# Low halves of the U blocks ahead of the gates: from GpSimd to VectorE

## The chip, the core and the metric

One NeuronCore of a Trainium2 chip runs the whole program. The metric is device time in microseconds (us). The engines are TensorE (PE, with its weight loads shown apart as PEld), VectorE (DVE), ScalarE (ACT), GpSimd (POOL) and SyncE (SP), which issues most of the DMAs. Each engine takes its instructions in the order in which they were placed on it.

## The reference, cut to what matters

One decoder layer over 512 tokens of width 1024: a token mixer (differential attention beside a gated linear recurrence), then PEER, a channel mixer that picks 128 experts per token out of 16384 by product keys. Only the second part matters here:

```python
q = jnp.einsum('nd,dc->nc', xb, w_query).reshape(PEER_BLOCK, PEER_HEADS, 2, PEER_QUERY_DIM // 2)
s = jnp.einsum('nhpc,hpkc->nhpk', q, subkeys).astype(jnp.float32)
sv, si = lax.top_k(s, PEER_TOPK)
...
top_s, pos = lax.top_k(cand_s, PEER_TOPK)
experts = jnp.take_along_axis(cand_i, pos, axis=-1).reshape(PEER_BLOCK, PEER_HEADS * PEER_TOPK)
gates = jax.nn.softmax(top_s, axis=-1).reshape(PEER_BLOCK, PEER_HEADS * PEER_TOPK)
u = u_table[experts]
hid = jax.nn.gelu(jnp.einsum('nkd,nd->nk', u, xb).astype(jnp.float32), approximate=False) * gates
return jnp.einsum('nk,nkd->nd', hid.astype(xb.dtype), v_table[experts])
```

## The kernel before

For the first three blocks of 128 tokens (ND = 3, 384 tokens) PEER is computed densely: all 16384 experts, in 128 blocks of 128 rows of U and V, with a dense matrix of gates that is zero where an expert was not picked. The last block of 128 tokens gathers its experts' rows instead.

fp32 products are made of three matmuls (`mm3`, L110 to L112) over operands that are split into a high and a low half. `split` (L105) lets ACT write the high half (L106) and VectorE or, where an engine is passed, that engine the low half (L107): `lo = src - hi`. `u_piece` loads 128 x 1024 numbers into `ur` (L655, SP's queue) and splits them into `uh` and `ul`; `ur`, `uh` and `ul` have three buffers each.

The part of the program around the change has these stages:

1. **Queries** (`s` from 0 to 15): TensorE multiplies a 128-column piece of the query weights (`ps_q`; these pieces are split with GpSimd), then scores (`pss`); VectorE picks the 16 largest of each list (`top16`, L736 to L740); GpSimd adds pairs of lists (`cand`, L763).
2. **Run-ahead and gates**: hidden values of the first 40 U blocks (RING = 40) are computed "ahead", in quarter steps (`run_ahead`, HP = 4), between the pieces of routing (`route`, L790 to L827) and the gate matmuls (`gates4`). A block is 24 matmuls into `ps_h` (two PSUM buffers), then a gelu on ACT into `hr` (L698). `gates4` makes two groups of one-hots on VectorE (`oh`, L837 and L843, three buffers), eight matmuls into `pgt` (L850, L851), and an ACT copy into `stg` (L852); there are 96 calls, 32 for each token block, and four steps of run-ahead go with five calls (RATE = 0.8). `stg` is stored to `g_dram`.
3. **Dense stage**: for each of 128 blocks the gates are read back (`gsl`, L975), a V block is loaded (`vr`, L977) and split, `hr` is multiplied by the gates (L982) and split (`wh`, `wl`), and 18 matmuls add into `y`; the hidden values of block `i + 40` follow. These U blocks are split with VectorE. VectorE also works on the gathered rows here (L912, L928).

A scheduler decides the order of instructions on each engine, from the program's order, the tiles' buffers and its own costs; only VectorE's order in the dense stage is the program's. Below, "gate" means one call of `gates4`, "block" one U block (24 matmuls), and "UL" one low half of a ring block (L107, `ul<-ur,uh`, 128x1024). UL0 is that of block 0.

Of the kernel before, what the change touches and what calls it, by code (L numbers as in the profile page):

```python
# [20 lines left out]
P = 128  # L21
# [16 lines left out]
ND = 3  # L38
# [2 lines left out]
GS = 2.0 ** 14  # L41
GB = 32
GI = 4
# sums of a pair of descending lists that can be among the 16 largest:
# (first row, rows, columns) of the blocks that cover (a + 1) * (b + 1) <= 16
CBLK = [(0, 1, 16), (1, 1, 8), (2, 2, 5), (4, 4, 3), (8, 8, 1)]
NCAND = sum(n * m for _, n, m in CBLK)
RING = 40
HP = 4
# [11 lines left out]
def tile_kernel(  # L61
# [25 lines left out]
    V, S, G, PE = nc.vector, nc.scalar, nc.gpsimd, nc.tensor  # L87
# [10 lines left out]
    V.memset(nhalf, -0.5)  # L98

    def rstd(dst, ssq, n, width):  # L100
        """dst = (ssq / n + eps) ** -0.5 for [P, width] tiles."""
        G.tensor_scalar(dst, ssq, 1.0 / n, EPS, op0=OP.mult, op1=OP.add)
        G.tensor_tensor(dst, dst, nhalf[: dst.shape[0], :width], op=OP.pow)

# [6 lines left out]
        PE.matmul(ps, ah, bl, start=False, stop=False)  # L111
        PE.matmul(ps, al, bh, start=False, stop=last)  # L112

    # ------------------------------------------------------------------ front
    with ExitStack() as fr:
        rstack = fr.enter_context(ExitStack())
        pa = fr.enter_context(tc.tile_pool(name="pa", bufs=8, space=PSUM))
# [4 lines left out]
        ssq = mixp.tile([P, NTB, 8], F32, name="ssq")  # L122
# [3 lines left out]
        with ExitStack() as pr:  # L126
# [35 lines left out]
            first = [pp.tile([P, HALF], F32, name="ps_t", tag="pa") for _ in range(4)]  # L162
# [56 lines left out]
                    f, *a = steps.pop(0)  # L219
                    f(*a)  # L220

            # ---- HGRN2 projections
            Q, QF, KR, FF = [], [], [], []
            w_second = w_piece(1)
            for xr in XR:
# [5 lines left out]
            second = [proj_t(w_second, 0, lo, hi) for lo, hi in halves]  # L231
# [20 lines left out]
            PE.transpose(prm, rv[:NMETA, NTB : NTB + 1].to_broadcast([NMETA, P]), ident[:NMETA, :NMETA])  # L252
            V.tensor_copy(rb[:, :NMETA], prm)

            # gates' lower bound: softmax over the two rows of logits, first row
            lg = fc.tile([P, 2, NH], F32, name="lg")
            nc.sync.dma_start(lg, lbl)
            lmx = fc.tile([P, NH], F32, name="lmx")
# [10 lines left out]
            for pc in range(2):  # L269
                for cb in range(2):  # L270
# [13 lines left out]
                    V.tensor_scalar(k, f, -1.0, 1.0, op0=OP.mult, op1=OP.add)  # L284
                    FF.append(f)
                    KR.append(k)
            # lambda
            lq = fc.tile([P, 4, 64], F32, name="lq")
            nc.sync.dma_start(lq.rearrange("p a b -> p (a b)"), row_bcast(lqk, 256))
            lsum = fc.tile([P, 2], F32, name="lsum")  # L290
# [29 lines left out]
            for pc in range(2):  # L320
                w = w_piece(2 + pc)
                for cb in range(2):
# [8 lines left out]
                    V.tensor_tensor(qf, q, FF[h][:, NMETA:], op=OP.mult)  # L331
                    Q.append(q)
                    QF.append(qf)
            # ---- HGRN2: scores inside the chunks, by a tree of decays
            AT = [hg.tile([P, NTB, P], F32, name=f"at{h}") for h in range(NH)]
            TOT = [(FF[h], NMETA) for h in range(NH)]

# [39 lines left out]
                run_one(vsteps)  # L377
            va, vam, vsteps = natural(12, "va", hp_)

            # ---- HGRN2: states at the chunks' starts and outputs  # L380
            def keys(h):
                k = KR[h]
                pk = pm.tile([P, 4, P], F32, name="pk", tag="pa")
# [47 lines left out]
            hstack.close()  # L431
            aqp = pr.enter_context(tc.tile_pool(name="aqp", bufs=1, reuse_waits="tile"))

            # ---- attention projections
            AQ, AK = [], []
            for which, lst, lo in ((8, AQ, NMETA), (10, AK, 0)):
                for pc in range(2):
                    w = w_piece(which + pc)
                    for cb in range(2):
                        n = T - lo  # L440
                        raw = tp.tile([P, T], F32, name="raw", tag="w2", bufs=W2)
                        segs = [(lo, T)] if n <= 512 else [(0, HALF), (HALF, T)]
                        for a, b in segs:
                            ps = proj_t(w, cb, a, b)
                            S.activation(raw[:, a - lo : b - lo], ps, AF.Copy, scale=0.125 if lo else 1.0)
                        rot = tp.tile([P, T], F32, name="rot", tag="w2", bufs=W2)
                        for g in range(4):
                            src = (g ^ 1) * 32
                            nc.sync.dma_start(rot[g * 32 : g * 32 + 32, :n], raw[src : src + 32, :n])
                        hh = pc * 2 + cb  # L450
                        V.tensor_tensor(rot[:, :n], rot[:, :n], sinr[:, lo:], op=OP.mult)
                        if lo:
                            # one query of the pair per half, zeros in the other
                            r = aqp.tile([P, 2, SEQ], F32, name=f"aq{hh}")
                            G.memset(r[64:, 0], 0.0)
                            G.memset(r[:64, 1], 0.0)
                            V.tensor_tensor(raw[:, :n], raw[:, :n], cosr[:, lo:], op=OP.mult)
                            for p2 in range(2):
                                r0 = slice(p2 * 64, p2 * 64 + 64)
                                V.tensor_tensor(r[r0, p2], raw[r0, :n], rot[r0, :n], op=OP.add)  # L460
                        else:
                            r = hp_.tile([P, T], F32, name=f"ak{hh}", tag=f"f{hh}")
                            V.tensor_tensor(r, raw, cosr, op=OP.mult)
                            V.tensor_tensor(r, r, rot, op=OP.add)
                        lst.append(r)
            # ---- attention core
            def scores(h, tb):
                nk = NMETA + (tb + 1) * P
                segs = [(0, nk)] if nk <= 512 else [(0, HALF), (HALF, T)]
# [57 lines left out]
                junk2 = tp.tile([P, P], F32, name="junk2", tag="junk2")  # L527
                S.activation(junk2, po, AF.Square, accum_out=ssq[:, tb, h : h + 1])

            # gate of the recurrence, times the norm's weight  # L530
            wg = {}

            def rg_step(i, tb):
# [108 lines left out]
            s1(SP)  # L642
            run_one(F)

        # ------------------------------------------------------ output projection
        xbp = ctx.enter_context(tc.tile_pool(name="xbp", bufs=1, reuse_waits="tile"))
        xbn_ = xbp.tile([P, D], F32, name="xbn")
        xbn_box.append(xbn_)
# [24 lines left out]
        s2(SP, 1)  # L673
        s3(2, X.pop(2), pm, "pa")

    # --------------------------------------------------------------- PEER
    ringp = ctx.enter_context(tc.tile_pool(name="ringp", bufs=RING, reuse_waits="tile"))
    ph = ctx.enter_context(tc.tile_pool(name="ph", bufs=2, space=PSUM, reuse_waits="tile"))
    spp = ctx.enter_context(tc.tile_pool(name="spp", bufs=1))
# [5 lines left out]
            pieces[i] = u_piece(uT[i], eng)  # L685

    def h_parts(i, eng=None, n=1):
        """gelu of block i's hidden values, in n steps; the last one appends it to the ring"""
        h_load(i, eng)
        if eng is not None and i + 1 < RING:  # L690
            h_load(i + 1, eng)
        uh, ul = pieces.pop(i)
        ps = ph.tile([P, DTOK], F32, name="ps_h", tag="ph")
        for kc in range(KC):
            mm3(ps, uh[:, kc], ul[:, kc], xbh[:, kc, :DTOK], xbl[:, kc, :DTOK], kc == 0, kc == KC - 1)
            if kc == KC - 1:
                hr = ringp.tile([P, DTOK], F32, name="hr", tag="hr")
                S.activation(hr, ps, AF.Gelu)  # L698
                ring.append(hr)
            if (kc + 1) % (KC // n) == 0:  # L700
                yield
# [3 lines left out]
    ring = []  # L705

    with ExitStack() as rt:
# [12 lines left out]
        starts = rc.tile([P, 16], I16, name="starts")  # L720
# [21 lines left out]
        for s in range(NSET):  # L742
            wh, wl = u_piece(wq[s], G) if s else qw_first
            ps = pq.tile([P, SEQ], F32, name="ps_q", tag="pq")
            parts = [slice(0, 256), slice(256, SEQ)] if s == 0 else [slice(0, SEQ)]
# [12 lines left out]
            if s % 2 == 1:  # L758
# [3 lines left out]
                for a0, na, nb in CBLK:  # L762
# [4 lines left out]
                        op=OP.add,  # L767
# [4 lines left out]

        qs.close()
        rw = rt.enter_context(tc.tile_pool(name="rg", bufs=2, reuse_waits="tile"))
        steps = (None for i in range(RING) for _ in h_parts(i, G, HP))

        def run_ahead(n):
            for _ in range(n):
                next(steps, None)

        def route(tb):
            # experts' two key indices
            idx = []

            def pick(which, sel, op, key, table, dt):
                """idx of the selected key: sum over a of op(sel, key[a]) * table[a]"""
                eq = rw.tile([P, PH * TOPK, TOPK], dt, name="eq", tag="eq", bufs=1)
                full = [P, PH * TOPK, TOPK]
                S.activation(eq, sel.rearrange("p h k -> p (h k)").unsqueeze(2).to_broadcast(full), AF.Copy)
                V.tensor_tensor(eq, eq, key.unsqueeze(1).to_broadcast(full), op=op)  # L790
                eqh = eq.rearrange("p (h k) a -> p h k a", h=PH)
                V.tensor_tensor(eqh, eqh, table.unsqueeze(2).to_broadcast([P, PH, TOPK, TOPK]), op=OP.mult)
                for w in (8, 4, 2):
                    V.tensor_tensor(eq[:, :, :w], eq[:, :, :w], eq[:, :, w : 2 * w], op=OP.add)
                ix = rw.tile([P, PH, TOPK], U32 if dt == I16 else F32, name=f"ix{which}")
                V.tensor_tensor(ix.rearrange("p h k -> p (h k)"), eq[:, :, 0], eq[:, :, 1], op=OP.add)
                return ix

            # first list: rank a is the last one whose candidates start at or before the position;
            # 64 * key + start comes out as a sum of the table's steps  # L800
            comb = rw.tile([P, PH, TOPK], I16, name="comb", bufs=1)
            step = rw.tile([P, PH, TOPK], I16, name="step", bufs=1)
            V.scalar_tensor_tensor(
# [10 lines left out]
            rank = rw.tile([P, PH, TOPK], F16, name="rank", bufs=1)  # L814
# [3 lines left out]
            idx = [ixa, pick(1, rank, OP.is_equal, io16, sif, F16)]  # L818
# [11 lines left out]
            return pmj  # L830

        def gates4(pmj, t0, stg, c0):
            """dense gates of four tokens: one-hots of the first key, of it times the gate's two parts, of the second"""
            oh = rw.tile([P, 4, P, 4], F16, name="oh", bufs=3)
            pgt = pg.tile([P, 4, P], F32, name="pgt", tag="pg")
            tq4 = slice(t0, t0 + 4)
# [4 lines left out]
                op=OP.is_equal,  # L841
# [5 lines left out]
                op=OP.mult,  # L847
# [4 lines left out]
            S.activation(stg[:, :, c0 : c0 + 4].rearrange("p i t -> p t i"), pgt, AF.Copy)  # L852

        run_ahead(16)
        # gates, in two parts of 11 bits for the dense blocks
        fl = "p t h k -> p (t h) k"
        mx = rc.tile([P, NTB * PH], F32, name="mx")
        V.tensor_copy(mx, TSA[:, :, :, 0].rearrange("p t h -> p (t h)"))
# [35 lines left out]
        for i in range(RING, RING + 1):  # L894
            h_load(i, G)

    # dense part for the first ND token blocks, gathered part for the last
    with ExitStack() as dn:
        dp = dn.enter_context(tc.tile_pool(name="dp", bufs=2, reuse_waits="tile"))
        gp = dn.enter_context(tc.tile_pool(name="gp", bufs=4, reuse_waits="tile"))  # L900
# [61 lines left out]
        last = []  # L962
        for i in range(NK):
# [31 lines left out]
            last = []  # L995
# [75 lines left out]
```

## Time and profile before

| what | value |
|---|---|
| three runs | 1656.32, 1657.58 (median), 1660.24 us |
| span of the profiled execution | 1655.8 us (median less span: 1.8 us) |
| busy over the span | PE 1595.0, DVE 1246.4, ACT 672.6, POOL 566.7 us |
| first ring matmul / first gate matmul / first `y` matmul | 441.56 / 517.13 / 751.38 us |

PE's busy time is a union of pipelined matmuls: one ring matmul is shown as about 334 ns long, while the next starts about 0.173 us after it. So PE's load is read from starts, not from busy time. PEclk is the granted clock of TensorE as a share of 2.4 GHz; its other level, 1.2 GHz, is 0.5.

### The profile page before, as it was taken

The page shows a single profiled execution, that of the slowest core. Times are in us where ns is not written, and L with a number is a line of the kernel's source. Part 1 is how long each engine was busy: PE and PEld are TensorE (multiplying, and loading weights), DVE is VectorE, ACT ScalarE, POOL GpSimd, SP SyncE. Part 2 cuts the span into 40 slices and gives each one's busy share as a digit, 9 for nine tenths or more (in the row PEclk, how much of TensorE's full clock was granted, in tenths as well). Part 3 has the DMA queues.
Part 4 walks back from the last instruction along what each step waited for, and adds up shares of the span by engine and source line. Part 5 has one row for each costly group of instructions (what it writes and reads, how often), then busy time and mean ns, then how long its engine had stood idle before and what let it go on. Part 6 is the DMA issues. An engine that isn't in the chain of part 4 may idle for free.

```text
span 1655.8 us, 23775 instructions
## 1 busy us (share of the span) xinstructions
PE 1595.0 (96%) x8859; PEld 1427.1 (86%) x8859; DVE 1246.4 (75%) x2375; ACT 672.6 (41%) x1017; POOL 566.7 (34%) x429
## 2 busy tenths in 40 slices
PE   7999998999978889999999999999999999999997
PEld 7899986888777889898999999999999999988886
DVE  6772568568898897837877778777777777767776
ACT  5123265422245666753433333333333333323333
POOL 2000012334444223254444444444444444433221
PEclk9999999999988999999999999999999999999999
DMA  6211322322222354569999988998898999877884
GB/s 205 77 50 45 118 71 103 115 90 77 73 81 100 143 203 174 207 228 357 337 322 319 324 306 308 318 323 309 311 331 304 318 321 314 311 233 262 282 278 144
DMA packets 145635, 363.93 MB, mean 220 GB/s; under 512 B 11888, under 2 KB 61296, under 8 KB 145392
## 3 DMA queue, kind: packets, MB, share of 16 engines
q1 hardware_dynamic: 107936, 227.10, 39.4%
q0 software_dynamic: 37008, 134.27, 23.4%
q8 instruction: 69, 1.13, 0.3%
q10 hardware_dynamic: 576, 1.05, 0.2%
q14 instruction: 46, 0.38, 0.1%
HBM read 330.92 MB, written 29.36 MB: 218 GB/s over the span
## 4 chain that ended last, share of the span: by engine, by line
PE 80%; DVE 13%; ACT 2%; DMA 1%; issue 1%; POOL 1%; SPq 0%; POOLq 0%; DVEq 0%; ACTq 0%
PE y L112 10%; PE y L111 10%; PE y L110 10%; PE ps_h L112 9%; PE ps_h L110 9%; PE ps_h L111 9%; PE pgt L850 2%; DVE oh L837 2%; PE pgt L851 2%; DVE oh L843 2%; PE ps_t L110 2%; PE ps_l L342 2%; PE ps_t L112 2%; PE ps_t L111 2%; PE ps_n L110 1%; PE ps_n L111 1%
## 5 line engine op out<-in xcount | busy, mean ns | idle before, releaser
L110 PE MATMUL ps_h<-xbh,uh 128*128 128x384 f32 x1024 | 355.1, 347 | 9.1 <-ACT hr L698 9.1
L112 PE MATMUL ps_h<-xbh,ul 128*128 128x384 f32 x1024 | 348.3, 340 | 3.3 <-POOL ul L107 3.3
L111 PE MATMUL ps_h<-xbl,uh 128*128 128x384 f32 x1024 | 347.6, 339 | 0.0
L110 PE MATMUL y<-vh,wh 128*128 128x512 f32 x768 | 299.0, 389 | 3.2 <-ACT wh L106 3.0
L112 PE MATMUL y<-vh,wl 128*128 128x512 f32 x768 | 300.9, 392 | 0.0
L111 PE MATMUL y<-vl,wh 128*128 128x512 f32 x768 | 300.4, 391 | 0.0
L922 POOL DMA_INDIRECT vg<-in_v_dram,exp_idx x128 | 185.3, 1448 | 277.8 <-DVE acc L928 210.6
L908 POOL DMA_INDIRECT ug<-in_u_dram,exp_idx x128 | 177.5, 1387 | 215.7 <-DVE jk L912 151.2
L107 DVE TENSOR_TENSOR vl<-vr,vh 128x1024 fp32r<-128x1024 f32 x128 | 156.8, 1225 | 123.0 <-ACT vh L106 121.1
L106 ACT ACTIVATE vh<-vr 128x1024 fp32r<-128x1024 f32 x128 | 136.0, 1062 | 266.2 <-issue 215.2
L106 ACT ACTIVATE uh<-ur 128x1024 fp32r<-128x1024 f32 x144 | 152.7, 1062 | 158.8 <-issue 69.4
L107 POOL TENSOR_TENSOR ul<-ur,uh 128x1024 fp32r<-128x1024 f32 x57 | 151.2, 2658 | 191.9 <-ACT uh L106 191.9
L110 PEld LDWEIGHTS ps_h<-xbh,uh 128*128 128x128 f32 x1024 | 197.2, 193 | 13.7 <-ACT hr L698 10.1
L111 PEld LDWEIGHTS ps_h<-xbl,uh 128*128 128x128 f32 x1024 | 196.3, 192 | 3.5
L112 PEld LDWEIGHTS ps_h<-xbh,ul 128*128 128x128 f32 x1024 | 195.3, 191 | 3.6 <-POOL ul L107 3.6
L110 PEld LDWEIGHTS y<-vh,wh 128*128 128x128 f32 x768 | 144.2, 188 | 31.9 <-ACT wh L106 4.2
L112 PEld LDWEIGHTS y<-vh,wl 128*128 128x128 f32 x768 | 144.1, 188 | 31.1 <-DVE wl L107 0.9
L111 PEld LDWEIGHTS y<-vl,wh 128*128 128x128 f32 x768 | 144.1, 188 | 28.3
L106 ACT ACTIVATE wh<-hr 128x384 fp32r<-128x384 f32 x128 | 67.2, 525 | 246.4 <-DVE hr L982 241.7
L928 DVE SCALAR_TENSOR_TENSOR acc<-vg,hid,acc 128x1024 f32<-128x1024 f32 x127 | 162.7, 1281 | 3.3 <-DMA vg<-in_v_dram,exp_idx 1.4
L912 DVE SCALAR_TENSOR_TENSOR jk<-ug,xbn 128x1024 f32<-128x1024 f32 x128 | 156.4, 1222 | 8.9 <-DMA ug<-in_u_dram,exp_idx 6.5
L107 DVE TENSOR_TENSOR wl<-hr,wh 128x384 fp32r<-128x384 f32 x128 | 71.5, 559 | 83.7 <-ACT wh L106 83.1
(268 smaller groups left out, 2716.5 us busy)
## 6 DMA issues: line engine op xcount, KB each, us to landing
ur<-in_uT_dram SPq DMA_DIRECT2D x128, 512.0 KB
vr<-in_v_dram SPq DMA_DIRECT2D x128, 512.0 KB
g_dram<-stg SPq DMA_DIRECT2D x48, 512.0 KB
gsl<-g_dram SPq DMA_DIRECT2D x32, 768.0 KB
wr<-in_w_in_dram SPq DMA_DIRECT2D x26, 512.0 KB
ur<-in_wq_dram SPq DMA_DIRECT2D x16, 512.0 KB
wor<-in_w_out_dram SPq DMA_DIRECT2D x8, 512.0 KB
xr<-in_xT_dram SPq DMA_DIRECT2D x8, 264.0 KB
```

The source lines that it names most:

```text
L106: S.activation(hi, src, AF.Copy)
L107: (eng or V).tensor_tensor(lo, src, hi.bitcast(F32), op=OP.subtract)
L110: PE.matmul(ps, ah, bh, start=first, stop=False)
L111: PE.matmul(ps, ah, bl, start=False, stop=False)
L112: PE.matmul(ps, al, bh, start=False, stop=last)
L342: PE.matmul(ps[:, c, :], KR[h][:, cs], rhs[:, c * P : c * P + P], start=True, stop=True)
L837: V.tensor_tensor(oh[:, :2], io128.unsqueeze(1).to_broadcast([P, 2, P, 4]), pmj[:, :2, tq4].unsqueeze(2).to_broadcast([P, 2, P, 4]), op=OP ...
L843: V.tensor_tensor(oh[:, 2:], oh[:, 0:1].to_broadcast([P, 2, P, 4]), pmj[:, 2:, tq4].unsqueeze(2).to_broadcast([P, 2, P, 4]), op=OP.mult,)
L908: G.indirect_dma_start(out=ug, out_offset=None, in_=u, in_offset=bass.IndirectOffsetOnAxis(ap=exp_idx[:, k : k + 1], axis=0))
L912: V.scalar_tensor_tensor(jk, ug, 1.0, xbn_, op0=OP.mult, op1=OP.mult, accum_out=hid[:, k : k + 1])
L922: G.indirect_dma_start(out=vg, out_offset=None, in_=v, in_offset=bass.IndirectOffsetOnAxis(ap=exp_idx[:, k : k + 1], axis=0))
L928: V.scalar_tensor_tensor(acc, vg, hid[:, k : k + 1], acc, op0=OP.mult, op1=OP.add)
```

## The change

`h_parts` no longer takes GpSimd for the 40 blocks that are run ahead, so `split` falls back to VectorE for their low halves. The test that loads and splits block `i + 1` before block `i` is multiplied hung on the engine that was passed; it now hangs on the number of steps (`n > 1`), so that the run-ahead keeps its look-ahead. The query pieces and block 40 stay on GpSimd, and the dense stage is as before. The other differences are removed comments.

```diff
     def h_parts(i, eng=None, n=1):
...
         h_load(i, eng)
-        if eng is not None and i + 1 < RING:
+        if n > 1 and i + 1 < RING:
             h_load(i + 1, eng)
...
-        steps = (None for i in range(RING) for _ in h_parts(i, G, HP))
+        steps = (None for i in range(RING) for _ in h_parts(i, None, HP))
```

Forty instructions leave GpSimd's queue and forty join VectorE's; the scheduler also places other work differently. VectorE's order at the end of the last `top16` and the start of routing (`tsa`: the scores' top 16, later the gates; `comb`, `step`, `eq`: routing's tables) was before:

```order
L858 COPY mx<-tsa 128x32
L739 MAX tsa<-t_4722 128x8
L740 MAX_INDEX ti_3463<-tsa,t_4722 128x8
L860 TENSOR_TENSOR tsa<-tsa,mx 128x512
L803 SCALAR_TENSOR_TENSOR comb<-si_3458,starts 128x128
...
L790 TENSOR_TENSOR eq<-eq,starts 128x2048
L792 TENSOR_TENSOR eq<-eq,step 128x2048
L794 TENSOR_TENSOR eq<-eq 128x128x8
```

and is now, at the same place:

```order
L107 TENSOR_TENSOR ul<-ur,uh 128x1024
L739 MAX tsa<-t_4722 128x8
L858 COPY mx<-tsa 128x32
L740 MAX_INDEX ti_3463<-tsa,t_4722 128x8
L107 TENSOR_TENSOR ul<-ur,uh 128x1024
L860 TENSOR_TENSOR tsa<-tsa,mx 128x512
...
L792 TENSOR_TENSOR eq<-eq,step 128x2048
L107 TENSOR_TENSOR ul<-ur,uh 128x1024
L794 TENSOR_TENSOR eq<-eq 128x128x8
```

These are UL4, UL5 and UL6. UL0 and UL1 stand in the two `top16` groups ahead of the last query pair, UL2 and UL3 at the end of that of `s = 15`, and UL7 to UL13 between the steps of routing; 14 ULs stand ahead of the first gate's one-hots, where there was none.

ACT's order at the same time (`hr` is the gelu that frees a PSUM buffer of TensorE, `eq` a copy that routing on VectorE waits for) was before:

```order
L698 ACTIVATE hr<-ps_h 128x384
L789 ACTIVATE eq<-ti_3463 128x2048
L106 ACTIVATE uh<-ur 128x1024
L698 ACTIVATE hr<-ps_h 128x384
L106 ACTIVATE uh<-ur 128x1024
L698 ACTIVATE hr<-ps_h 128x384
L861 ACT_TABLE_LOAD
```

and is now:

```order
L698 ACTIVATE hr<-ps_h 128x384
L106 ACTIVATE uh<-ur 128x1024
L698 ACTIVATE hr<-ps_h 128x384
L789 ACTIVATE eq<-ti_3463 128x2048
L106 ACTIVATE uh<-ur 128x1024
L698 ACTIVATE hr<-ps_h 128x384
L861 ACT_TABLE_LOAD
```

One high half and one gelu moved ahead of the first `eq`. On PE, 313 ring matmuls (13.04 blocks) now stand ahead of the first gate matmul instead of 264 (11 blocks), and five instead of six blocks follow the last gate.

In the gates, VectorE's order just after the sixteenth one-hot group of the first token block, where routing of the second is made, was before:

```order
L843 TENSOR_TENSOR oh<-oh,pmj 128x1024
L813 CAST ixa<-k_5518 128x128
L815 TENSOR_TENSOR rank<-ti_3461,ix_5516 128x128
L837 TENSOR_TENSOR oh<-io_3432,pmj 128x1024
L806 COPY step<-comb 128x8
L807 TENSOR_TENSOR step<-comb 128x8x15
L843 TENSOR_TENSOR oh<-oh,pmj 128x1024
L837 TENSOR_TENSOR oh<-io_3432,pmj 128x1024 x2
L790 TENSOR_TENSOR eq<-eq,io_3431 128x2048
```

and is now:

```order
L843 TENSOR_TENSOR oh<-oh,pmj 128x1024
L794 TENSOR_TENSOR eq<-eq 128x128x8
L107 TENSOR_TENSOR ul<-ur,uh 128x1024
L794 TENSOR_TENSOR eq<-eq 128x128x4
L107 TENSOR_TENSOR ul<-ur,uh 128x1024
L794 TENSOR_TENSOR eq<-eq 128x128x2
L107 TENSOR_TENSOR ul<-ur,uh 128x1024
L796 TENSOR_TENSOR ix_5516<-eq 128x128
L837 TENSOR_TENSOR oh<-io_3432,pmj 128x1024
L810 TENSOR_SCALAR k_5518<-ix_5516 128x128
L843 TENSOR_TENSOR oh<-oh,pmj 128x1024
```

The first half of this routing now comes behind the sixteenth group, with three ULs in it, and its second half runs between the next five gates instead of ahead of them. Everywhere else in the gates one UL stands between an L837 and its L843, once for about five gates.

## Rows read from the trace of the kernel before

**Rows 1.** Stretches around the ring: us and instructions of PE, PEld, DVE, ACT, POOL; PEclk; DMA

```profile
441.00:517.00 76.00, 57.15 (x280) 55.00 (x278) 66.72 (x240) 29.99 (x32) 33.20 (x22) 0.82 0.23 77
517.00:751.00 234.00, 219.71 (x1474) 203.15 (x1472) 179.15 (x225) 147.62 (x160) 83.58 (x33) 0.99 0.52 190
550.00:570.00 20.00, 15.87 (x90) 14.86 (x90) 15.47 (x18) 9.42 (x10) 7.72 (x3) 0.83 0.51 181
590.00:620.00 30.00, 25.71 (x181) 23.16 (x180) 26.71 (x34) 18.10 (x20) 7.58 (x3) 1.00 0.52 193
751.00:1656.00 905.00, 895.37 (x4416) 800.18 (x4416) 706.37 (x877) 333.20 (x455) 363.81 (x264) 1.00 0.86 301
```

**Rows 2.** Waits of PE, 440 to 750: total us, times, longest

```profile
PE ps_h L110 <- ACT hr L698: 9.1, 3, 5.3
PE pgt L850 <- DVE oh L843: 7.5, 16, 1.6
PE ptp L827 <- DVE ixa L813: 6.5, 1, 6.5
PE ptp L827 <- DVE ix L796: 4.1, 1, 4.1
```

**Rows 3.** The tile ul: ns min/median/max, first and last start

```profile
L107 DVE TENSOR_TENSOR ul<-ur,uh x87: 1210/1218/1221, 758.3 to 1466.0; 128x1024 fp32r<-128x1024 f32 x87
L107 POOL TENSOR_TENSOR ul<-ur,uh x57: 2343/2412/5164, 312.8 to 742.5; 128x1024 fp32r<-128x1024 f32 x57
```

**Rows 4.** Timeline of VectorE, 470 to 515: start, us, what, [idle before <-releaser]

```profile
470.81 3.28 DVE L792 TENSOR_TENSOR eq<-eq,step 128x2048 int16<-128x2048 int16 x1
...
505.99 1.22 DVE L792 TENSOR_TENSOR eq<-eq,sif 128x2048 f16<-128x2048 f16 x1
507.25 0.69 DVE L794 TENSOR_TENSOR eq<-eq 128x1024 f16<-128x1024 f16 x1
...
514.25 3.48 DVE L843 TENSOR_TENSOR oh<-oh,pmj 128x1024 f16<-128x1024 f16 x2
```

**Rows 5.** Timeline of GpSimd, VectorE and ACT, 448 to 476

```profile
448.20 2.34 POOL L107 TENSOR_TENSOR ul<-ur,uh 128x1024 fp32r<-128x1024 f32 x1
450.84 0.34 DVE L736 MAX8 tsa<-cand 128x8 f32<-128x54 f32 x2 [1.93 <-POOL cand L763]
467.61 1.91 ACT L789 ACTIVATE eq<-ti 128x2048 int16<-128x2048 uint32 x1 [9.03 <-DVE ti L740]
470.55 5.77 POOL L107 TENSOR_TENSOR ul<-ur,uh 128x1024 fp32r<-128x1024 f32 x2 [4.23 <-ACT uh L106]
```

**Rows 6.** Timeline of a steady stretch of the gates: GpSimd, VectorE, PE

```profile
666.46 2.89 POOL L107 TENSOR_TENSOR ul<-ur,uh 128x1024 fp32r<-128x1024 f32 x1 [6.46 <-ACT uh L106]
667.35 2.55 DVE L837 TENSOR_TENSOR oh<-io,pmj 128x1024 f16<-128x1024 f16 x1 [0.25 <-PE pgt L851]
668.22 0.29 PE L850 MATMUL pgt<-oh 128*128 128x128 f16 x1
...
670.56 0.28 PE L850 MATMUL pgt<-oh 128*128 128x128 f16 x1 [0.17 <-DVE oh L843]
...
672.56 0.28 PE L850 MATMUL pgt<-oh 128*128 128x128 f16 x1
...
675.77 2.90 POOL L107 TENSOR_TENSOR ul<-ur,uh 128x1024 fp32r<-128x1024 f32 x1 [6.42 <-ACT uh L106]
```

**Rows 7.** Timeline of PE: first of a group of three ring matmuls, and three groups on

```profile
479.89 0.33 PE L110 MATMUL ps_h<-xbh,uh 128*128 128x384 f32 x1
...
481.45 0.33 PE L110 MATMUL ps_h<-xbh,uh 128*128 128x384 f32 x1
```

**Rows 8.** Timeline of the ring's end: VectorE, ACT, PE

```profile
719.81 0.69 DVE L843 TENSOR_TENSOR oh<-oh,pmj 128x1024 f16<-128x1024 f16 x1
...
747.50 1.06 ACT L106 ACTIVATE vh<-vr 128x1024 fp32r<-128x1024 f32 x1 [6.13 <-DMA vr<-in_v_dram]
751.38 0.50 PE L110 MATMUL y<-vh,wh 128*128 128x512 f32 x1 [3.03 <-ACT wh L106]
```

## The prediction

> **What bounds the kernel now.** I read the busy times by stage first. From 751 us to the end TensorE is busy 895.4 of 905 us at full clock [rows 1]: that stage is TensorE's own, the change doesn't touch its code, and a microsecond won before it reaches the end whole. So only the stretch from the first ring matmul (441.6) to the first `y` matmul (751.4, [rows 8]) counts: 309.8 us.
>
> How much of it is work? Three groups of three ring matmuls take 481.45 - 479.89 = 1.56 us [rows 7], so a block (eight groups) is 8 x 0.52 = 4.16 us and 40 blocks are 166.4. In the steady gates one period, from one low half on GpSimd to the next, is 675.77 - 666.46 = 9.31 us [rows 6] and holds five gates and one block: (9.31 - 4.16) / 5 = 1.03 us a gate, 98.9 for 96. That leaves 309.8 - 265.3 = 44.5 us, of which I put some 5 on scores and transposes. About 40 us are lost. The windows say where: TensorE sits idle 76 - 57.2 = 18.8 us before the first gate and 234 - 219.7 = 14.3 behind it, and ahead of the first gate its mean clock is 0.82, so some 0.36 of that time lies at 1.2 GHz [rows 1].
>
> Then I asked who is waited for. TensorE waits 9.1 us for gelu copies on ACT, 6.5 and 4.1 for routing results of VectorE, and 7.5 in 16 pieces for one-hots [rows 2]. The first is VectorE's too: ACT's `eq` copy stood 9.03 us waiting for the top 16 [rows 5], with the gelus behind it in ACT's queue. So before the gates VectorE's chain (top 16, softmax, routing) ends last; in the steady gates TensorE does.
>
> And VectorE's chain is slowed by GpSimd. The multiplication at L792 took 3.28 us beside GpSimd's low halves (470.55, for 5.77 us) and 1.22 at 505.99, the sum at L794 0.69 when nothing ran there [rows 4, 5]. In the gates, L837 took 2.55 us and ended at 669.90, 0.55 behind the low half that had begun at 666.46; the usual one-hot takes 0.69 [rows 6, 8]. A low half on GpSimd costs VectorE nearly 2 us when they meet. The Trainium skill says why (SBUF — State Buffer, Who interferes with whom): a VectorE instruction with two SBUF inputs shares a read port with GpSimd and waits for the whole of an instruction there. The trace agrees.
>
> **The change, part by part.** A low half takes 1.22 us on VectorE and 2.41 (median) on GpSimd [rows 3]. Forty of them add 40 x 1.22 = 48.8 us to VectorE and take 40 x 2.41 = 96 from GpSimd, which is not waited for in the end. What counts is what they displace.
>
> *Ahead of the first gate.* 14 ULs join VectorE's chain: +17.1 us. What goes: seven instructions between 470 and 517 that met GpSimd (first and last: L792 at 470.81, the pair L843 at 514.25 with 3.48 against 2 x 0.69). Their excess is 3.28 - 1.22 = 2.06 for the first and 3.48 - 1.38 = 2.10 for the last [rows 4, 8], so about 7 x 2.1 = 14.7. Also the 1.93 us in which VectorE waited for `cand`, queued behind a low half [rows 5]; GpSimd has only `cand` there now. Balance: 17.1 - 14.7 - 1.9 = +0.5 us. One new wait comes in: UL5 needs `uh5`, which needs block 2 off its buffer, and UL2 and UL3 are made only when the last `top16` is nearly over, so TensorE has nothing between blocks 1 and 2, and `hr2` now stands ahead of the first `eq` on ACT. I put +1.5 us on it: the `eq` can start about when block 2 is evicted. The first gate then comes at about 519 instead of 517.1. But by then 13.04 blocks are multiplied, not 11: 2.04 x 4.16 = 8.5 us of TensorE's work is out of the way. Can they be fed? From the first `eq` (467.6) to the first gate nine ULs are made in about 50 us, one for 5.5 us, slower than the 4.16 that TensorE needs, but with blocks 2 to 4 in hand. Term: -8.5 + 2 = **-6.5 us**. Bounds: the first gate 1.5 us earlier than before (if the ACT wait falls into time in which VectorE waited for ACT anyway), -10; if those long instructions are not shortened at all, 14.7 more: +8.2.
>
> *Routing of the second token block* (550 to 570). Here TensorE lost 20 - 15.9 = 4.1 us, and the clock of 0.83 over 20 us [rows 1] means 0.34 of it, 6.8 us, at the lower level, half of that lost: 3.4. Together 7.5. Now five gates stand between the two halves of this routing. I count VectorE from the sixteenth one-hot to the `ixa` that TensorE waits for: sums 0.69 + 0.45 + 0.42, three ULs 3.66, two results 0.43 + 0.67, one gate 1.38, in all 7.7; TensorE has one gate and 1.12 blocks, 1.03 + 4.66 = 5.7, so it waits 2.0. Term: 7.5 - 2.0 = **-5.5**. Bounds -7.5 and 0.
>
> *Routing of the third* (590 to 620): 30 - 25.7 = 4.3 lost [rows 1]. By the same count, VectorE has 10.3 us to the next `ixa` (two multiplications 2.44, two ULs 2.44, sums 1.56, two gates 2.76, the results 1.1), and TensorE one gate and 1.8 blocks, 8.5: it waits 1.8. Term: **-2.5**, bounds -4.3 and 0.
>
> *Steady gates.* A period with a low half loses a little each time: from 668.22 to 670.56 a gate and a quarter block take 2.34 us, from 670.56 to 672.56 without it 2.00 [rows 6]. 0.34 x 20 periods = 6.8. The UL now delays the same one-hots, by 1.22 where it was 2.55 - 0.69 = 1.86. VectorE then needs 5 x 1.38 + 1.22 = 8.1 us of a period of 9.0, and each UL's high half stands several gates ahead of it on ACT. I take half: **-3**; bounds -6.8 and 0.
>
> *Ring's end.* VectorE ended the last one-hots at 720.5, `y` began at 751.4: 31 us, of which TensorE waited the last 3.03, because `vr` landed only at 747.5 [rows 8]. Five blocks (20.8 us) instead of six follow now. The loads stand behind the same stores, but the `ur` loads ahead of them on SP no longer wait for low halves at GpSimd's pace, since VectorE has nothing else there. I take **0**; bounds -3 (the wait goes) and +4 (one block less to hide the loads, nothing gained).
>
> Sum: -6.5 - 5.5 - 2.5 - 3 + 0 = -17.5 us. The profiled execution has 1655.8 us of span, 1.8 below the median of the runs; 1655.8 - 17.5 + 1.8 = 1640.1. I say **1640**. Behind 751 nothing is to be won: VectorE's and GpSimd's order there is the same.
>
> **Rivals.** *A. VectorE becomes the bound, slower.* It is busy 66.7 of 76 us ahead of the first gate [rows 1], and the new instructions stand in its one queue, where everything behind them waits. If the long instructions are long for another reason than GpSimd, the first gate comes 8.2 + 8.5 = 16.7 us late, and the two blocks won give 8.5 back: 1657.6 + 8.2 = 1666. It decides from the point at which less than about 6 of the 14.7 us of excess go away. Against it: short and long cases of the same instruction stand 35 us apart, and differ in whether GpSimd was at work [rows 4, 5]. The Trainium skill speaks for this rival (Perfetto Trace Analysis, Optimizing Scalar/DVE Operations): a saturated VectorE is to be relieved, even towards GpSimd; the same paragraph warns that the two share a read port. By the first half the change costs, by the second it doesn't; the traces favour the second. 15%.
>
> *B. Given back at the ring's end.* If the loads of the dense stage keep their 31 us from the last one-hots, the blocks won early only make TensorE wait there: five blocks and a gate are 21.8 us, six were 26, so 4.2 go: 1644; and if routing still holds the gates back as before (no -5.5, no -2.5), 1652. For it: `y` already waits 3 us. 15%, around 1650.
>
> *C. Hidden anyway.* GpSimd is not the bound, and the new waits of VectorE for ACT's high halves eat the steady and routing terms, and as much again in the first: 1656 to 1658. For it: ACT holds gelus, `eq` and high halves in one queue, and once waited 9 us there [rows 5]. 10%.
>
> *D. More.* If blocks are fed so well that the lower clock vanishes too, the 0.36 x 76 = 27 us at 1.2 GHz give back another 8 or so beyond the terms: 1631. Against it: UL2 comes late. 10%.
>
> **How the numbers follow.** The forecast, 50%, has its own range of 1633 to 1650. With D's 1631 inside and C's 1658 and about a third of A reached, 8 in 10 lie in 1630 to 1660. 0.2% is 3.3 us, about what a measurement of this kernel can tell from no change. Faster: the forecast, D and B, 75%; same: C, 10%; slower: A, 15%.
>
> **What would show it.** In the changed profile: GpSimd without `ul` between 436 and 742 but for block 40; L792, L794 and L837 without lengths of 2.5 us and more; `ul` on VectorE at about 1.22; the first gate matmul at 517 to 521 with 313 ring matmuls ahead of it; TensorE's busy time around the two routings at 9 of 10 or more; `y` at 730 to 738. I am wrong if VectorE stands waiting for ACT's `uh` ahead of its ULs, if TensorE's clock ahead of the gates falls well below 0.82, or if `y` waits for `vr` by much more than 3 us.

## The result, and the profile after

The changed kernel takes 1633.99 us (median; 1632.69 to 1634.34), the kernel before 1656.95 on the same chip (1655.16 to 1660.24): 0.986 of it, 95% interval 0.9847 to 0.9873. The span is 1632.6 us after 1655.8, and nearly all of the gain lies ahead of the first `y` matmul: it starts at 729.99 instead of 751.38 us, 21.4 earlier. The last 1.8 us come behind it.

The busy times by stage, of the changed kernel (columns as in [rows 1]: window, its length, busy us of PE, PEld, DVE, ACT, POOL, granted clock, DMA share, GB/s):

```profile
441.00:515.00 74.00, 60.21 (x331) 58.45 (x330) 66.18 (x252) 33.80 (x37) 3.28 (x10) 0.93 0.29 100
512.00:706.00 194.00, 189.36 (x1310) 175.53 (x1309) 160.28 (x250) 137.61 (x146) 0.00 (x0) 0.98 0.48 177
520.00:550.00 30.00, 27.70 (x181) 25.59 (x180) 25.29 (x42) 19.00 (x21) 0.00 (x0) 0.89 0.39 151
550.00:570.00 20.00, 20.00 (x140) 18.54 (x140) 16.90 (x27) 16.84 (x19) 0.00 (x0) 1.00 0.44 158
590.00:620.00 30.00, 29.37 (x204) 27.69 (x202) 27.00 (x44) 19.94 (x21) 0.00 (x0) 1.00 0.54 200
...
525.00:530.00 5.00, 3.70 (x29) 3.23 (x27) 4.46 (x7) 3.07 (x5) 0.00 (x0) 0.76 0.33 129
530.00:535.00 5.00, 5.00 (x26) 4.53 (x24) 2.96 (x5) 2.69 (x3) 0.00 (x0) 0.56 0.98 358
```

TensorE idles 13.8 us ahead of the first gate, where it was 18.8, at a clock of 0.93 for 0.82; the two holes of the routings (15.87 of 20 and 25.71 of 30 in [rows 1]) are closed. VectorE is busy for 66.2 us ahead of the first gate, as before (66.7), though it makes 14 low halves more. A new hole stands at 520 to 550, at a clock of 0.89, most of which belongs to the ten microseconds of the last two lines. The second line, from the first to the last one-hot, is read further below.

The tiles `oh` and `ul` of the changed kernel (ns min/median/max, first and last start):

```profile
L850 PE MATMUL pgt<-oh x384: 274/297/330, 514.5 to 708.9; 128*128 128x128 f16 x192
L837 DVE TENSOR_TENSOR oh<-io,pmj x96: 669/685/705, 512.5 to 703.3; 128x1024 f16<-128x1024 f16 x96
L843 DVE TENSOR_TENSOR oh<-oh,pmj x96: 672/684/706, 513.7 to 705.0; 128x1024 f16<-128x1024 f16 x96
...
L107 DVE TENSOR_TENSOR ul<-ur,uh x127: 1201/1218/1228, 442.7 to 1443.2; 128x1024 fp32r<-128x1024 f32 x127
L107 POOL TENSOR_TENSOR ul<-ur,uh x17: 2371/2392/2420, 312.2 to 722.2; 128x1024 fp32r<-128x1024 f32 x17
```

None of 192 one-hots is long any more. The same lines of the kernel before say what they were, and how long the gates took:

```profile
L850 PE MATMUL pgt<-oh x384: 275/297/302, 517.1 to 722.9; 128*128 128x128 f16 x192
...
L837 DVE TENSOR_TENSOR oh<-io,pmj x96: 673/686/2823, 513.0 to 719.1; 128x1024 f16<-128x1024 f16 x96
L843 DVE TENSOR_TENSOR oh<-oh,pmj x96: 667/684/2884, 514.2 to 719.8; 128x1024 f16<-128x1024 f16 x96
```

So the first gate is 2.6 us earlier, the stretch from the first to the last gate 194.4 us instead of 205.8 (-11.4), and from the last gate to `y` it is 21.1 instead of 28.5 (-7.4): together the 21.4.

TensorE's waits from 440 to 740 (total us, times, longest), to be read against [rows 2]; the waits for one-hots are gone, and a new one leads:

```profile
PE ps_h L112 <- DVE ul L107: 12.4, 3, 9.4
PE ps_h L110 <- ACT hr L698: 5.3, 7, 1.3
PE ptp L827 <- DVE ixa L813: 1.1, 1, 1.1
PE ptp L827 <- DVE ix L796: 0.3, 1, 0.3
```

The timeline of the changed kernel has the place of the 9.4 us: UL2, the low half of the third block, is made only at 462.41, behind a `top16`, and that block's first matmul that needs it (L112) waits until then. The first `eq`, which the prediction saw coming when block 2 is evicted, starts at 471.66.

```profile
462.41 1.21 DVE L107 TENSOR_TENSOR ul<-ur,uh 128x1024 fp32r<-128x1024 f32 x1
463.68 0.69 PE L112 MATMUL ps_h<-xbh,ul 128*128 128x384 f32 x1 [9.41 <-DVE ul L107]
...
470.32 1.06 ACT L106 ACTIVATE uh<-ur 128x1024 fp32r<-128x1024 f32 x1 [14.38 <-PE ps_h L111]
471.42 1.22 DVE L107 TENSOR_TENSOR ul<-ur,uh 128x1024 fp32r<-128x1024 f32 x1 [1.72 <-ACT uh L106]
471.66 1.90 ACT L789 ACTIVATE eq<-ti 128x2048 int16<-128x2048 uint32 x1
```

### The profile page after: what moved, and what is told of

Same layout as the page of the kernel before. It is cut to its first block, busy times and chain, and to the rows that moved or that the text cites. A ratio compares the mean times of both kernels' runs of the same rounds, so it can differ in the third digit from the quotient of the medians.

```text
span 1632.6 us, 23785 instructions
## 1 busy us (share of the span) xinstructions
PE 1586.8 (97%) x8859; PEld 1422.3 (87%) x8859; DVE 1230.8 (75%) x2415; ACT 673.7 (41%) x1017; POOL 457.6 (28%) x389
## 4 chain that ended last, share of the span: by engine, by line
PE 87%; DVE 7%; ACT 3%; POOL 1%; issue 1%; DMA 1%; SPq 0%; POOLq 0%; DVEq 0%; ACTq 0%
PE ps_h L110 11%; PE y L111 11%; PE y L112 11%; PE ps_h L112 11%; PE y L110 11%; PE ps_h L111 10%; PE pgt L850 3%; PE pgt L851 3%; PE ps_t L110 2%; PE ps_l L342 2%; PE ps_t L112 2%; PE ps_t L111 2%; PE ps_n L110 2%; PE ps_n L111 2%; PE ps_n L112 1%
## 5 line engine op out<-in xcount | busy, mean ns | idle before, releaser
L112 PE MATMUL ps_h<-xbh,ul 128*128 128x384 f32 x1024 | 347.5, 340 | 12.4 <-DVE ul L107 12.4
L110 PE MATMUL ps_h<-xbh,uh 128*128 128x384 f32 x1024 | 349.1, 341 | 5.3 <-ACT hr L698 5.3
L112 PE MATMUL y<-vh,wl 128*128 128x512 f32 x768 | 300.6, 391 | 0.0
L112 PEld LDWEIGHTS ps_h<-xbh,ul 128*128 128x128 f32 x1024 | 194.1, 190 | 13.4 <-DVE ul L107 13.4
L110 PEld LDWEIGHTS ps_h<-xbh,uh 128*128 128x128 f32 x1024 | 194.4, 190 | 10.9 <-ACT hr L698 7.5
L111 PEld LDWEIGHTS ps_h<-xbl,uh 128*128 128x128 f32 x1024 | 194.4, 190 | 3.5
L112 PEld LDWEIGHTS y<-vh,wl 128*128 128x128 f32 x768 | 144.1, 188 | 30.4
L107 DVE TENSOR_TENSOR ul<-ur,uh 128x1024 fp32r<-128x1024 f32 x127 | 154.7, 1218 | 11.3 <-ACT uh L106 10.9
```

The lines of the kernel that those rows point to most:

```text
L107: (eng or V).tensor_tensor(lo, src, hi.bitcast(F32), op=OP.subtract)
L110: PE.matmul(ps, ah, bh, start=first, stop=False)
```

## The experiments

All times are medians, and each ratio is to the kernel before on the same chip. The edits are to the changed kernel.

**GpSimd works again, for nothing.** VectorE still makes all low halves, and GpSimd makes seven eighths of each once more, into a tile that nobody reads. If the meetings are the cause, they come back.

```diff
             split(h, l, r, eng)
+            junk and G.tensor_tensor(pst.tile([P, KC - 1, P], F32, name="uj", bufs=1),
+                r[:, 1:], h[:, 1:].bitcast(F32), op=OP.subtract)
...
-            pieces[i] = u_piece(uT[i], eng)
+            pieces[i] = u_piece(uT[i], eng, i < RING)
```

> The changed kernel, in which GpSimd also computes 7/8 of each ring block's low half (128x896) into a tile that nobody reads. Order on every other engine is that of the changed kernel. Theory (the gain is that GpSimd no longer holds up VectorE's two-input instructions): routing's instructions and one-hots that meet GpSimd lengthen to 2.3 to 3.3 us again, the first gate comes 8 to 15 us later, and the time is 1644 to 1659 us. Rival (the gain is the other order and the faster supply of low halves, not the meeting): those instructions keep about 1.2 and 0.7 us, and the time stays within 1634 to 1638 us.

1676.0 us, 1.0101 of before (1.0081 to 1.0121): some 40 us slower than the changed kernel, more than the theory's 1644 to 1659. Its timeline (line numbers are one higher in this kernel and the next) shows GpSimd, then the second one-hots of two gates (L844) and TensorE behind them:

```profile
656.45 12.64 POOL L659 TENSOR_TENSOR uj<-ur,uh 128x896 f32<-128x896 f32 x3 [8.81 <-ACT uh L106]
664.53 5.12 DVE L844 TENSOR_TENSOR oh<-oh,pmj 128x1024 f16<-128x1024 f16 x2
667.20 0.29 PE L851 MATMUL pgt<-oh 128*128 128x128 f16 x1 [0.88 <-DVE oh L844]
669.71 0.29 PE L851 MATMUL pgt<-oh 128*128 128x128 f16 x1 [1.22 <-DVE oh L844]
```

Two one-hots take 5.12 us beside GpSimd where the pair takes 1.28 alone, and TensorE waits for each. Not every meeting does this. The first of the three GpSimd instructions in the top row takes 7.6 us, and VectorE's one-hots beside it, up to 662 us, keep their usual 0.7; the other two take 2.4 each and hold up the two one-hots.

Nobody reads the tile. GpSimd's extra reading could also keep the buffers of `ur` and `uh` from the next blocks, but a high half on ACT waits for it only once, for 3.5 us. What grows is VectorE's busy time, with the same instructions: 80.6 us for 63.2 up to the first one-hot, and in the gates 191.2 for 160.3:

```profile
532.00:748.00 216.00, 196.49 (x1309) 179.46 (x1308) 191.21 (x250) 137.97 (x146) 75.88 (x23) 0.95 0.43 159
```

So this is the price of GpSimd's being at work. It costs more than in the kernel before because VectorE now carries both: the low halves and the meetings.

**GpSimd only writes.** In its place GpSimd clears the loaded tile twice for each block, when both halves are made: it writes SBUF and reads nothing.

```diff
             split(h, l, r, eng)
+            for _ in range(2 if junk else 0):
+                G.memset(r[:, 1:], 0.0)
...
-            pieces[i] = u_piece(uT[i], eng)
+            pieces[i] = u_piece(uT[i], eng, i < RING)
```

> The changed kernel, in which GpSimd sets 7/8 of each ring block's loaded tile to zero, twice, after both halves were made: GpSimd is busy in the same stretch as in e1, but it only writes and reads nothing. The order on the other engines is nearly that of the changed kernel (28 of VectorE's rows stand elsewhere). Theory (what holds VectorE up is GpSimd reading operands through a port that VectorE's second input needs): one-hots and routing keep 0.7 and 1.2 us, and the time is 1633 to 1642 us. Rival (any work of GpSimd holds VectorE up): one-hots of 1.5 us and more, 1650 us or more.

1636.75 us, 0.9872 (0.9856 to 0.9889). The clears overlap one-hots, which keep their lengths, as GpSimd and VectorE in its timeline show:

```profile
649.80 1.76 POOL L659 MEMSET ur<- 128x896 f32 x2 [8.32 <-DVE ul L107]
650.27 1.28 DVE L838 TENSOR_TENSOR oh<-io,pmj 128x1024 f16<-128x1024 f16 x2
```

Of the 192 one-hots 65 overlap a clear, and the longest of all is 718 ns; a clear takes 0.85 us, so one that had to be waited for would show. So what holds VectorE up is not that GpSimd is busy but that it reads. The Trainium skill has this rule (SBUF — State Buffer, Who interferes with whom): a VectorE instruction with two SBUF inputs contends with a GpSimd instruction that reads SBUF, not with one that only writes it. The trace agrees, for 80 clears.

**Only the early low halves on VectorE** (0 to 13; the 26 in the gates stay on GpSimd), and **only the late ones** (the other way round).

```diff
+        pick = lambda j: G if n > 1 and j >= 14 else eng     # late: j < 14
-        h_load(i, eng)
+        h_load(i, pick(i))
...
-            h_load(i + 1, eng)
+            h_load(i + 1, pick(i + 1))
```

> Low halves 0 to 13 on VectorE, 14 to 39 on GpSimd. Theory: the part of the gain ahead of the first gate stays (first gate at about 514.5 us with some 13 blocks ahead of it) and the part in the gates goes (about 9 to 10 us): 1643 to 1645 us. Rival (all of the gain is the early part): 1634 to 1637 us.

> Low halves 0 to 13 on GpSimd, 14 to 39 on VectorE. Theory: the first gate is back at about 517 us with 11 blocks ahead of it, the part in the gates stays: 1643 to 1647 us. Rival (all of the gain is in the gates): 1634 to 1637 us.

Early alone: 1659.57 us, 0.9997 (0.9988 to 1.0007), nothing. Late alone: 1640.2 us, 0.9884 (0.9867 to 0.99), 19 us. Both expectations missed: the early part is worth nothing by itself, and the late part more than its theory said, though not quite all as its rival had it. The busy times of the stretch from the first to the last one-hot tell why. That of the kernel before:

```profile
513.00:721.00 208.00, 196.36 (x1336) 180.27 (x1335) 181.46 (x227) 137.34 (x147) 69.90 (x24) 0.98 0.48 175
```

That of the kernel with the early low halves alone:

```profile
512.00:721.00 209.00, 189.27 (x1276) 173.14 (x1276) 182.79 (x227) 134.13 (x143) 68.26 (x22) 0.95 0.46 167
```

And that of the kernel with the late ones alone; the changed kernel's is the second line of the first table:

```profile
511.00:710.00 199.00, 197.97 (x1376) 184.44 (x1374) 166.21 (x250) 141.53 (x151) 5.93 (x2) 1.00 0.49 181
```

The early kernel does what the prediction wanted of it: it has 313 ring matmuls (13.04 blocks) behind it at the first gate, instead of 264 (11), and that gate comes at 516.5. But VectorE's work in the gates is what it was, 182.8 us for 181.5, and the stretch takes as long (209 for 208 us) although TensorE has two blocks less to do in it (20.96 for 23, counted matmul by matmul). The last gate starts at 722.9 in both. The two blocks won early became idle time of TensorE (19.7 us in the stretch for 11.6), as its waits from 440 to 740 show:

```profile
PE pgt L850 <- DVE oh L843: 12.8, 17, 2.1
PE ps_h L112 <- DVE ul L107: 11.1, 2, 8.6
PE ptp L827 <- DVE ix L796: 5.5, 2, 5.2
PE ptp L827 <- DVE ixa L813: 2.8, 2, 1.7
```

That is 12.8 us for one-hots, 7.5 in [rows 2], and the clock of the stretch fell from 0.98 to 0.95. In the late kernel VectorE has 15 us less and TensorE is full, 197.97 of 199 us: there the bound has changed engines.

**Without the look-ahead.** The other half of the diff, alone undone.

```diff
-        if n > 1 and i + 1 < RING:
-            h_load(i + 1, eng)
```

> The changed kernel without the look-ahead: block i+1 is loaded and split in the program when block i is done. Theory (the look-ahead keeps the high and low half, 1.06 and 1.22 us, out of TensorE's way, though the scheduler can put them early by itself; it has two free buffers): 2 to 10 us slower than the changed kernel, 1636 to 1644 us. Rival (each of the 40 blocks waits for its own split, 2.3 us less what the second PSUM buffer hides): 1665 us or more; other rival (the scheduler finds the same order): 1634 to 1636 us.

1631.6 us, 0.9836 (0.9819 to 0.9852). The expectation missed: the clause that the change keeps alive is worth nothing here. The first gate came at 514.0, and TensorE waited about as long for low halves (13.2 us for 12.4).

**The first four low halves left to GpSimd**, against the late UL2; then three and six.

```diff
+        pick = lambda j: G if n > 1 and j < 4 else eng     # 3, 6
-        h_load(i, eng)
+        h_load(i, pick(i))
...
-            h_load(i + 1, eng)
+            h_load(i + 1, pick(i + 1))
```

> Low halves 0 to 3 on GpSimd, where only the top-16 instructions with one tensor input run beside them; 4 to 39 on VectorE. Theory: those four are not in VectorE's way (3.7 to 4.9 us of its chain) and TensorE no longer waits 12.4 us for low halves 0 to 2, of which half counts: 1626 to 1630 us. Rival (TensorE's early waits are slack because VectorE's chain to the first gate ends last, and the top 16 are held up by GpSimd like routing): 1633 to 1637 us.

> Low halves 0 to 2 on GpSimd, the rest on VectorE. Theory (e4's gain is VectorE's chain to the first gate being shorter by one low half for each that moves, as long as the top 16 run beside it): about 1.2 us slower than e4, 1629 to 1633 us. Rival (the gain is TensorE's 9.4 us wait for low half 2, which is gone here too): the same as e4 within 0.5 us.

> Low halves 0 to 5 on GpSimd, the rest on VectorE. Theory: low halves 4 and 5 meet the softmax and routing on VectorE there, so each costs some 2 us where it saves 1.2: 1 to 4 us slower than e4, 1630 to 1634 us. Rival (VectorE's load alone counts, not the meeting): 2 to 3 us faster than e4, 1626 to 1628 us.

Four: 1629.2 us, 0.9817 (0.98 to 0.9833). Three: 1631.93, 0.9843 (0.9827 to 0.9859). Six: 1629.94, 0.9826 (0.9809 to 0.9842), just under its theory's 1630, with one L792 held up again (3282 ns). Three and six are not told apart from four, so whether the gain is the wait for UL2 or VectorE's shorter chain stays open. With four, TensorE's waits from 440 to 740 are these; the 9.4 us for UL2 are gone, and the 9.4 that lead now are gelu copies:

```profile
PE ps_h L110 <- ACT hr L698: 9.4, 6, 6.3
PE ps_h L112 <- POOL ul L107: 3.3, 1, 3.3
```

Its first gate starts at 507.8, with 12 blocks ahead of it, and the window 520 to 550 has no hole and the full clock:

```profile
520.00:550.00 30.00, 29.95 (x205) 28.22 (x204) 27.74 (x44) 21.34 (x23) 0.00 (x0) 1.00 0.57 211
```

**On one chip: the changed kernel, the version with four, and that without the look-ahead.**

> The changed kernel itself, beside the next two on one chip, as their measure. Every theory: 0.984 to 0.988 of the kernel before, about 1633 us.

> Low halves 0 to 3 on GpSimd, the rest on VectorE, again, beside the changed kernel on the same chip. If the early low halves on VectorE delay the second block, as the trace of the changed kernel reads, this version is 4 to 7 us faster than the changed kernel on this chip, at a ratio of 0.980 to 0.984. If the gap was the chip's, it is within 2 us of it.

> The same version without the lines that split the next block early. If these lines are worth nothing, as the run without them showed, within 3 us of the version with them; if they only were of no use because the first blocks were late, 3 us or more slower than it.

| kernel | median, lowest to highest | ratio, interval |
|---|---|---|
| changed | 1631.98, 1631.73 to 1632.40 | 0.9855, 0.9838 to 0.9872 |
| four on GpSimd | 1628.19, 1627.37 to 1629.85 | 0.9835, 0.9820 to 0.9850 |
| the same, no look-ahead | 1624.85, 1624.54 to 1625.20 | 0.9811, 0.9796 to 0.9825 |

No two ranges of times overlap, five runs each (four of the changed kernel). Four on GpSimd gain 3.8 us on the changed kernel, just under the 4 that the expectation set as its lower end. Without the look-ahead it is another 3.3 us faster, which neither side of that expectation held: the clause is not worth nothing but less. TensorE's waits in its trace:

```profile
PE ps_h L110 <- ACT hr L698: 6.9, 3, 6.3
PE ps_h L112 <- POOL ul L107: 3.3, 1, 3.3
PE ptp L827 <- DVE ixa L813: 1.7, 1, 1.7
```

And the stretch of its gates, in which TensorE is busy for all but 0.7 us:

```profile
505.00:694.00 189.00, 188.33 (x1317) 172.77 (x1316) 161.44 (x250) 138.67 (x147) 0.00 (x0) 1.00 0.49 182
```

With the look-ahead TensorE waited three times more for `hr`, 2.5 us in all (9.4 in 6). The code would have it so: the look-ahead puts the next high half on ACT ahead of the gelu copy. That this is the whole of the 3.3 us is argued, not shown. This is the fastest version found.

## Why the prediction was right, and where it wasn't

The sum was -17.5 us (1640), the measurement -23: inside the range, in the forecast's own (1633 to 1650, at its lower end). The mechanism held. The sizes of the terms did not, and that the sum still came near is in part luck: some were too small, one too large. By place, with TensorE's work counted as the prediction counts it, the change gave 11.1 us ahead of the first gate (forecast 6.5), 8.3 in the gates (11), 3.2 at the ring's end (0), and 0.6 behind the first `y` (0), where another 1.2 are seven matmuls of block 40 that now stand ahead of it.

**GpSimd's low halves hold VectorE up, some 2 us a meeting: right.** In the gates VectorE's busy time fell from 181.5 to 160.3 us although 23 low halves (27.1 us) came in: 48.3 us of holding went with 24 low halves on GpSimd, 2.0 each. Ahead of the first gate the seven long instructions lost 14.9 us, for a forecast of 14.7: there 14 low halves (17.0 us) came in, and VectorE's busy time is about what it was. The two experiments that give GpSimd needless work show the cause: reading brings the long instructions back, writing doesn't. Rival A (VectorE becomes the bound) failed at its condition: all of the excess went, not less than 6 of 14.7. (By the prediction's own sum its first term turns at 8.2, not at 6.)

**Ahead of the first gate, -6.5: mis-sized, and wrongly priced.** The matmul count was exact (313), but the first gate came at 514.5, not at about 519: by the prediction's own count 2.6 + 8.5 = 11.1 us of gain, just beyond its bound of 10. The first `eq` did come late, by 4.1 us (471.66 for 467.61), and yet the 1.5 us set down for it did not show: VectorE's waits for `eq` up to the first one-hot fell from 6.4 to 4.2 us.

The price was wrong too: a block that is out of the way early counts 4.16 us only if TensorE is what ends last afterwards. With the gates' low halves still on GpSimd, the same blocks were worth nothing (0.9997). On top of the late ones they gave 0.9884 - 0.986 = 0.0024, about 4 us, and these two intervals just overlap. UL2 was late, as foreseen, and held TensorE up for 9.4 us. Leaving four low halves to GpSimd removes that wait and gave 3.8 us; as it also takes 4.9 us out of VectorE's chain, how much of the 3.8 is the wait's is not shown.

**Routings and steady gates, -5.5 - 2.5 - 3 = -11: too small for what the late low halves are worth.** Alone they gave 19 us, 14.7 of them between the first and the last gate (196.3 us with 24.25 blocks instead of 205.8 with 23). What failed is the step from "in the steady gates TensorE does" end last to all of the gates. In the steady gates it does, but the first 56 of the 96 aren't steady: VectorE makes the routings of the next two token blocks there. The two parts, of the kernel before:

```profile
517.00:650.00 133.00, 122.82 (x829) 113.29 (x828) 113.72 (x147) 86.92 (x93) 46.70 (x17) 0.97 0.44 159
650.00:721.00 71.00, 69.54 (x487) 63.01 (x485) 63.74 (x77) 48.98 (x53) 20.89 (x8) 1.00 0.57 208
```

And of the kernel with the early low halves alone:

```profile
517.00:650.00 133.00, 116.80 (x775) 107.37 (x773) 113.99 (x147) 82.90 (x88) 43.43 (x14) 0.92 0.42 150
650.00:721.00 71.00, 69.57 (x488) 63.08 (x486) 63.80 (x77) 49.11 (x53) 20.96 (x8) 1.00 0.57 208
```

In the second part TensorE is busy 69.5 of 71 us at full clock in both. In the first the early kernel's TensorE has two blocks less to do, is busy for 6 us less and at a lower clock, and gains nothing: the 57th gate starts at 649.6 us instead of 649.5, with 26.25 blocks done in both. VectorE's work is the same there, 114.0 for 113.7 us. It isn't full either; in the kernel before it waits 16.7 us of the 133 for TensorE to free one-hot buffers. The two engines waited for each other in turn, so that a held-up one-hot could cost both. So in that part the shortening of VectorE's chain counted, not half of TensorE's small waits. The same shows in the third routing's term: the 4.3 us that TensorE lost from 590 to 620 were three waits for held-up one-hots, not for `ixa`.

By place, the changed kernel took less out of the gates than forecast: the stretch from first to last gate is 11.4 us shorter with 22.25 blocks in it instead of 23; less 0.75 x 4.16 = 3.1 us for these, 8.3 us of lost time went. The routings' holes did close (20.00 of 20 and 29.37 of 30 us, clock 1.00). TensorE waits for no result of theirs any more, where 2.0 and 1.8 us were forecast; the waits of 1.1 and 0.3 us further above stand ahead of the first gate. But from 520 to 550 a loss came in that the kernel before hadn't: 27.70 of 30 us at 0.89, for 28.75 at 1.00.

**Ring's end, 0: it gained.** Of the 7.4 us from the last gate to `y`, 4.2 are the one block less. The wait of 3.03 us before `y` is gone, the lower bound of the term. `y` came 24.3 us after the last one-hots (705.7), not 30.9, so the loads did not keep their distance: rival B is refuted. The first `vr` load was issued at 716.4 us instead of 736.1, 19.7 earlier, where the last one-hots were 14.8 earlier. Rival C (hidden) fell with the measurement. D's 1631 was nearer than 1640, and a part of its way came true: the clock ahead of the first gate rose from 0.82 to 0.93, while that of 520 to 550 fell. How much that gave was not separated; in the early kernel the clock rose as well (0.92 up to the first gate) and the time did not change.

Of the signs to look for, those on lengths, on GpSimd's queue (one `ul` left, at 722.2), on the 313 matmuls and on the routings came out; the first gate was 2.5 us earlier than 517, and `y` at the edge of 730 to 738. One sign of being wrong came out as well: VectorE did stand waiting for ACT's `uh` ahead of its ULs, five times, for 10.9 us in all (longest 4.0), and the gain came in spite of it.

## What to carry to other kernels

If long cases of a two-input VectorE instruction coincide with a GpSimd instruction that reads SBUF, count VectorE's time with the excess removed before deciding which engine is full: here 40 low halves moved onto the busier engine made it less busy. Where two engines hand buffers to each other, neither looks full and both wait; time won by one ahead of such a stretch is worth its price only when the other keeps up inside it, so take the parts of a change apart before adding their terms. And give the first few pieces, for which a long queue on the target engine makes others wait, to the engine that is idle there.

## What the runs showed of the hardware that I had not expected

GpSimd's reading held up fp32 low halves on VectorE too, not only fp16 one-hots. The tile `ul` on VectorE where GpSimd made them once more, and the GpSimd instruction itself:

```profile
L107 DVE TENSOR_TENSOR ul<-ur,uh x127: 1199/1218/3143, 442.6 to 1485.4; 128x1024 fp32r<-128x1024 f32 x127
...
L659 POOL TENSOR_TENSOR uj<-ur,uh x40: 2090/2956/7638, 435.0 to 758.7; 128x896 f32<-128x896 f32 x40
```

VectorE's longest is 1.9 us above its median, as for the one-hots, and GpSimd's is held up as well: its median is 2956 ns for a shortest of 2090, and its longest 7638.

And TensorE's clock fell with gates and blocks at hand: in the changed kernel it was granted 0.76 from 525 to 530 us and 0.56 to 535, which is mostly its lower level of 1.2 GHz. TensorE had been busy for 4.73 of 5 us from 505 to 510 and for all of the next 15, and stood still for 1.30 us, ahead of 527.91, for a gelu copy. In a second run of the changed kernel the same wait (1.29 us) stands at 526, and the clock from 525 to 530 was 0.66. In the version with four low halves on GpSimd, which has no such wait there, it stayed at 1.00. Why it fell was not settled.
